# Squares summed ahead of their product, and norm and modulation steps in another order, in a two-block transformer kernel

## The chip, the cores and the metric

The kernel runs on one core of a Trainium2 chip. The metric is device microseconds for one execution of the whole program. The engines are named as the profile names them: PE (TensorE, matrix products), PEld (its weight loads), DVE (VectorE), ACT (ScalarE), POOL (GpSimd) and SP (the queue that issues most DMAs).

## The reference

Two transformer blocks run one after the other on one sequence of 512 tokens of width 1024. The change touches the first block only. Cut to what matters, it computes

```
mod = silu(c) @ w_ada + b_ada                      # 6 vectors of 1024: shift1, scale1, gate1, shift2, scale2, gate2
h   = rms_norm(x, g_norm1) * (1 + scale1) + shift1
proj = h @ w_in                                    # q, k, v of the stick-breaking heads; q, k, v, o, gates of the mLSTM
q, k = rms_norm per head of 64                     # 8 heads
y_sb = stick_breaking(q, k, v);  y_ml = mlstm(...)
x   = x + gate1 * (concat(y_sb, y_ml) @ w_out)
h2  = rms_norm(x, g_norm2) * (1 + scale2) + shift2
x   = x + gate2 * peer(h2)                         # scores, two top-k stages, 16384 experts with tables u and v

rms_norm(x, g) = x * rsqrt(mean(x*x) + eps) * g
```

## The kernel before

The residual `xT` is held transposed: 8 tiles of 128 features by 512 tokens. Products keep float32 accuracy by splitting each operand into a rounded part and a rest: `cut` makes `whi` (a cast, mostly on ACT, L151) and `wlo` (a subtraction on DVE or POOL, L152) from a weight tile of 128x1024, `split` does the same to an activation, and `mm3` issues three products (L171 with `wlo`, L172 with the rest of the activation, L173 with both rounded parts). So a product that uses a weight tile waits for both its `whi` and its `wlo`.

A norm needs the sum of squares over the features, which lie on partitions: `square` (L1145, L1146) squares one tile on ACT and multiplies it by a matrix of ones on PE, which adds up the partitions and, over the 8 tiles, the features in one PSUM bank. `rstd` (from L192) then does one step from PSUM on DVE (L198, `rs_m`), a Ln and an Exp on ACT (L199, L200), and three steps on DVE (L203 to L205). With `split=True` the last three are handed back as a function, to be called later.

Everything the change touches lies inside `manual_schedule` sections, in which the order of the program text is the order that was chosen by hand for each engine's queue. Three stretches matter.

**The start** (`start`, 0 to 110 us). `silu(c)` is spread over partitions by 8 small products with a diagonal (`dg`, L1210) and copied to `cs` by ACT (L1213). Then come the 8 squares and their products, the cut of the first weight tile, and two `dot`s on DVE (L1195) that multiply a row tile of `w_ada` with `cs` and give 128 elements of scale and 128 of shift. Then a loop over the 8 feature tiles i runs:

```
fetch(i + 2)          # two tiles of w_ada, one of i_qk (SP)
dot(KD + i + 1)       # DVE, scale of the next tile
low(i)                # DVE, hl: the rest of the normed tile i
dot(i + 1)            # DVE, shift of the next tile
shape(i + 1)          # DVE: 2 small steps and mt; ACT: hh; then the next cut: ACT whi, POOL wlo
24 products of tile i # PE
```

`low(i)` needs `hh` of tile i, which ACT makes from `mt`. After the loop, 96 products give the values of the heads, in 8 groups `kk`; between the groups `normed` norms one tile of q or k each, in the order 0, 4, 1, 5, 2, 6, 3, 7: a product with a block matrix (L1280), `rs_m` on DVE, Ln and Exp on ACT, and a group later `finish` (L203 to L205 and L1285 on DVE). As soon as tiles 0 and 4 are done, `stack(0)` splits the first two heads into the operands of their scores: 4 copies on ACT, 2 on DVE, 4 subtractions on POOL (L1351 to L1355). The values are copied out of PSUM by ACT at the end (L1312, `vs`), and the stick-breaking section begins with the score products `z` (L1444).

**The end of the mixer** (`mlstm`, 378 to 407 us). 8 projections of `w_out` (`project("b", ...)`), each 12 products; in turn with them DVE does the dots of shift2 and scale2 (L1134) and adds each result to `xT` (L1639), ACT and PE do `square`, and POOL makes the `wlo` of the next weight tiles. At the end `rstd` makes the second norm's factor.

**The start of the routing** (`peer` and `route`, from 407 us). `cut_u(0)` cuts the first tile of the expert table u (`whi` on DVE at L149, `wlo` on POOL). `modulated` (from L1148) norms and modulates the 8 tiles: per tile a multiplication on DVE (L1161, `mt`), two passes on ACT (L1162, L1163, the second gives `phh`), a copy of the first 128 tokens on POOL (L1165, `h2t`), and the rest `phl` on DVE (L1156). Then the loop over 16 query tiles begins. Its first round issues the products of query tile 0 feature by feature, and after every second feature pulls one piece of the expert products out of a queue of fillers:

```
for k in range(KD):
    c.mm3(ps, ...)            # query tile 0, feature k
    if i == 0 and k % 2:
        fill.pull(1)          # 6 products of tile u(0), with features k-1 and k
```

The functions that the diff touches, and what calls them:

Of the kernel before, what the change touches and what calls it, by code (L numbers as in the profile page):

```python
# [20 lines left out]
P = 128  # L21
# [1077 lines left out]
class Block1:  # L1099
# [48 lines left out]
    def modulated(self, rstd, gname, shift, scale, hi, lo, keep=None, bufs=2):  # L1148
# [5 lines left out]

        def low(k):
            nc.vector.tensor_tensor(out=lo[:, k], in0=ts[k], in1=hi[:, k].bitcast(F32), op=ALU.subtract)  # L1156

        for k in range(KD):
            t = self.sm.tile([P, S], F32, tag="mt", bufs=bufs, name=c.name("mt"))
            ts.append(t)  # L1160
            nc.vector.tensor_tensor(out=t, in0=self.xT[:, k], in1=rstd, op=ALU.mult)  # L1161
            nc.scalar.activation(t, t, AF.Identity, scale=a[:, k:k + 1], bias=self.mod[:, shift + k:shift + k + 1])  # L1162
            nc.scalar.copy(hi[:, k], t)  # L1163
            if keep is not None:
                nc.gpsimd.tensor_copy(keep[:, k], t[:, :P])  # L1165
            if k > 1:
                low(k - 2)
# [3 lines left out]
    def start(self, wk, hh, hl, q, k, vs, gq, stack):  # L1171
# [34 lines left out]
        cs = [self.bank() for _ in range(2)]  # L1206
        for j in range(KD):
            d = dg[:, j * P:(j + 1) * P]
            nc.vector.tensor_scalar(d, c.ident, ct[:, j:j + 1], None, op0=ALU.mult)
            mm(cs[j // 4][:, j % 4 * P:(j % 4 + 1) * P], lhsT=c.ones, rhs=d, start=j % 4 == 0, stop=True,  # L1210
               skip_group_check=True)
        for i in range(2):
# [4 lines left out]
        pn = self.bank()  # L1217
        for j in range(KD):
            self.square(pn, j)
# [5 lines left out]
        rstd = c.rstd(self.sm, pn, [P, S], D, EPS1, "hrstd", bufs=2)  # L1225
# [3 lines left out]
        def shape(i):  # L1229
            nc.vector.tensor_scalar(mod[:, KD + i:KD + i + 1], mod[:, KD + i:KD + i + 1], up[:, i:i + 1],  # L1230
                                    c.col("g1", i), op0=ALU.add, op1=ALU.mult)
            nc.vector.tensor_scalar(mod[:, i:i + 1], mod[:, i:i + 1], c.col("b_ada", i), None, op0=ALU.add)
            ts[i] = self.sm.tile([P, S], F32, tag="mt", name=c.name("mt"))
# [9 lines left out]

        shape(0)
        for i in range(KD):
            fetch(i + 2)
            if i + 1 < KD:
                dot(KD + i + 1)
                low(i)
                dot(i + 1)  # L1250
                shape(i + 1)
# [25 lines left out]
        def normed(j):  # L1277
# [6 lines left out]
            def finish():  # L1284
                nc.vector.scalar_tensor_tensor(out=dst[m], in0=dst[m], scalar=gq if m < 4 else c.col("gk"),  # L1285
                                               in1=rest(), op0=ALU.mult, op1=ALU.mult)
                if m == 4:
                    stack(0)
# [5 lines left out]
        for k0 in range(0, KD, 2):  # L1294
# [3 lines left out]
            for kk in range(k0, k0 + 2):  # L1298
                s0 = slice((kk - k0) * 512, (kk - k0 + 1) * 512)
                if kk % 2 == 0 and k0 + 2 < KD:  # L1300
                    vcut[k0 + 2] = c.cut(vraw.pop(k0 + 2), 1024, None, nc.gpsimd)
                for b in range(NB):
# [247 lines left out]
    def mlstm(self, m2, wk, big, hh, hl, vm, ym, qk, og, rows, identb, closing):  # L1550
# [200 lines left out]
        with self.psum(bank=7, norm=1):  # L1751
            pn = self.bank("norm")
            for m in range(KD):
# [4 lines left out]
                if m:  # L1758
                    self.square(pn, m - 1)
# [3 lines left out]
            self.square(pn, KD - 1)  # L1763
            self.rstd = c.rstd(self.sm, pn, [P, S], D, EPS1, "prstd", self.st, bufs=2)

    def peer(self):
# [7 lines left out]
        with ExitStack() as ctx:  # L1774
# [62 lines left out]
            with tc.manual_schedule():  # L1837
                fetch_u(1)
                cut_u(0)
# [550 lines left out]
```

## Time and profile before

| what | value |
|---|---|
| median of 3 runs | 3176.5 us (3174.7 to 3179.04) |
| the profiled execution's own time | 3176.89 us |
| its span in the profile | 3175.0 us |
| PE busy | 2967.8 us, 93% of the span |
| DVE busy | 2143.1 us, 67% |
| ACT busy | 1289.8 us, 41% |
| POOL busy | 662.1 us, 21% |

The profile is of one execution. Its span runs from the first to the last instruction, and the execution's own time adds what lies around it. Busy shares are means over very different stages: the stretches that the change touches are less than 200 us of the span, and what counts in them is which wait ends last. In a timeline each line gives the start, the duration, the engine, the line, the operation, the tiles, and in brackets how long the engine had stood idle and whom it waited for; an operation that is held up after it was issued shows a longer duration instead.

### The profile page before, as it was taken

The numbers are of one execution on the slowest core, as the hardware profiler recorded it, in microseconds if no ns is written. First come the engines' busy times: TensorE is split into PE (matmuls) and PEld (weight loads), VectorE is DVE, ScalarE is ACT, GpSimd is POOL, SyncE is SP. The second block draws the span as 40 slices with busy tenths as digits, with TensorE's granted clock in tenths as the row PEclk, the third lists the DMA queues.
The fourth block names the chain that finished last, engine by engine and source line by source line (L and its number), as shares of the span: only waits on it lengthen the run. The fifth ranks groups of instructions, "written<-read, shape, count | busy, mean of one in ns | idle before, by whom it ended". The sixth has DMA issues, their size and how long they took to land.

```text
span 3175.0 us, 44359 instructions
## 1 busy us (share of the span) xinstructions
PE 2967.8 (93%) x17073; PEld 2588.8 (82%) x17073; DVE 2143.1 (67%) x4089; ACT 1289.8 (41%) x2356; POOL 662.1 (21%) x453
## 2 busy tenths in 40 slices
PE   8889987858999999999999999989999988999998
PEld 6666577758899999999998777689999966798896
DVE  6886667789777778777786647755445666555454
ACT  3764342237533333333333334433233367433232
POOL 4432134630112112111110234330000322300001
PEclk9989899879999999999999999999999999899999
DMA  6222321215888888888887311022232311122322
GB/s 217 73 74 100 105 88 67 77 50 220 327 312 301 320 304 302 317 305 311 307 290 241 106 60 41 30 72 94 81 100 81 99 33 34 54 87 86 101 88 85
DMA packets 160805, 479.29 MB, mean 151 GB/s; under 512 B 13489, under 2 KB 68657, under 8 KB 142546
## 3 DMA queue, kind: packets, MB, share of 16 engines
q1 hardware_dynamic: 139346, 316.03, 29.9%
q0 software_dynamic: 18432, 134.23, 11.4%
q10 hardware_dynamic: 2816, 26.22, 2.0%
q8 instruction: 134, 2.20, 0.3%
q14 instruction: 77, 0.63, 0.1%
HBM read 449.15 MB, written 27.27 MB: 150 GB/s over the span
## 4 chain that ended last, share of the span: by engine, by line
PE 72%; DVE 14%; issue 6%; POOL 3%; ACT 3%; DMA 1%; SPq 0%; DVEq 0%; POOLq 0%; ACTq 0%
PE big L171 8%; PE big L173 8%; PE big L172 8%; PE y L172 5%; PE y L173 5%; PE y L171 5%; PE u L171 5%; PE u L173 5%; PE u L172 5%; POOL wlo L152 2%; PE bank L2233 2%; PE s L536 1%; PE f L171 1%; PE bank L172 1%; PE bank L171 1%
## 5 line engine op out<-in xcount | busy, mean ns | idle before, releaser
L152 DVE TENSOR_TENSOR wlo<-wraw,whi 128x1024 fp32r<-128x1024 f32 (+2 forms) x409 | 479.6, 1173 | 531.6 <-ACT whi L151 528.8
L151 ACT CAST whi<-wraw 128x1024 fp32r<-128x1024 f32 (+3 forms) x530 | 524.3, 989 | 702.3 <-PE y L173 267.6
L171 PE MATMUL big<-xh,wlo 128*128 128x264 f32 (+2 forms) x1408 | 422.5, 300 | 4.8 <-POOL wlo L152 4.5
L173 PE MATMUL big<-xh,whi 128*128 128x264 f32 (+2 forms) x1408 | 420.6, 299 | 0.0
L172 PE MATMUL big<-xl,whi 128*128 128x264 f32 (+2 forms) x1408 | 419.8, 298 | 0.0
L152 POOL TENSOR_TENSOR wlo<-wraw,whi 128x1024 fp32r<-128x1024 f32 (+4 forms) x122 | 270.6, 2220 | 689.7 <-ACT whi L151 652.1
L171 PE MATMUL u<-phh,wlo 128*128 128x384 f32 x1024 | 353.7, 345 | 57.3 <-POOL wlo L152 33.2
L173 PE MATMUL u<-phh,whi 128*128 128x384 f32 x1024 | 349.8, 342 | 0.0
L172 PE MATMUL u<-phl,whi 128*128 128x384 f32 x1024 | 349.6, 341 | 0.0
L1887 POOL DMA_INDIRECT g<-in_uv,idx x128 | 159.9, 1249 | 819.0 <-DVE yg L1901 451.1
L173 PE MATMUL y<-whi,ph 128*128 128x512 f32 x768 | 301.1, 392 | 0.0
L172 PE MATMUL y<-wlo,ph 128*128 128x512 f32 x768 | 300.9, 392 | 0.0
L171 PE MATMUL y<-whi,pl 128*128 128x512 f32 x768 | 299.1, 389 | 1.5 <-DVE pl L167 1.5
L171 PEld LDWEIGHTS big<-xh,wlo 128*128 128x128 f32 x1408 | 266.6, 189 | 15.2 <-POOL wlo L152 6.0
L172 PEld LDWEIGHTS big<-xl,whi 128*128 128x128 f32 x1408 | 267.1, 190 | 8.1
L173 PEld LDWEIGHTS big<-xh,whi 128*128 128x128 f32 x1408 | 266.5, 189 | 7.8
L171 PEld LDWEIGHTS u<-phh,wlo 128*128 128x128 f32 x1024 | 198.0, 193 | 67.4 <-POOL wlo L152 38.0
L172 PEld LDWEIGHTS u<-phl,whi 128*128 128x128 f32 x1024 | 197.6, 193 | 4.3
L173 PEld LDWEIGHTS u<-phh,whi 128*128 128x128 f32 x1024 | 196.9, 192 | 0.0
L171 PE MATMUL big<-ah,wlo 128*128 128x264 f32 (+2 forms) x539 | 171.4, 318 | 1.9 <-DVE wlo L152 1.7
L172 PE MATMUL big<-al,whi 128*128 128x264 f32 (+2 forms) x539 | 170.8, 317 | 0.0
L173 PE MATMUL big<-ah,whi 128*128 128x264 f32 (+2 forms) x539 | 170.8, 317 | 0.0
(503 smaller groups left out, 6305.6 us busy)
## 6 DMA issues: line engine op xcount, KB each, us to landing
wraw<-in_ut SPq DMA_DIRECT2D x128, 512.0 KB, 6.0
wraw<-in_uv SPq DMA_DIRECT2D x128, 512.0 KB, 5.7
wraw<-in_f_in SPq DMA_DIRECT2D x88, 512.0 KB, 3.3
gscratch<-stage ACTq DMA_DIRECT2D x12, 2048.0 KB, 6.8
gt<-gscratch SPq DMA_DIRECT2D x32, 768.0 KB, 8.3
wada<-in_w_ada SPq DMA_DIRECT2D x40, 512.0 KB, 3.6
wraw<-in_f_out SPq DMA_DIRECT2D x32, 384.0 KB, 3.1
wraw<-in_f_out SPq DMA_DIRECT2D x32, 320.0 KB, 2.9
```

Of the source, the lines that this page charges most:

```text
L151: self.nc.scalar.copy(hi[:, :n], raw[:, :n])
L152: (engine or self.nc.vector).tensor_tensor(out=lo[:, :n], in0=raw[:, :n], in1=hi[:, :n].bitcast(F32), op=ALU.subtract)
L171: mm(out, lhsT=wl, rhs=xh, start=first, stop=False)
L172: mm(out, lhsT=wh, rhs=xl, start=False, stop=False)
L173: mm(out, lhsT=wh, rhs=xh, start=False, stop=last)
L536: mm(o[:, :n], lhsT=q[:, rows(b)], rhs=k[:, k0:k0 + n], start=True, stop=True)
L1887: nc.gpsimd.indirect_dma_start(out=g, out_offset=None, in_=t["uv"], in_offset=bass.IndirectOffsetOnAxis(ap=idx[:, k:k + 1], axis=0))
L2233: nc.tensor.matmul(ps[:, e * P:(e + 1) * P], lhsT=b[:, e], rhs=a[:, e], start=e == 0, stop=True, skip_group_check=True)
```

## The change

- In `start`, the squares come ahead of the copies of `cs`, in pairs: POOL adds the two squares of a pair, and PE multiplies the 4 sums by the ones instead of 8 squares, each product standing between the small products of `dg`.
- Still in `start`, the two small steps of `shape` become `scales`; those of tile 0 come ahead of `rstd`; and `low(i)` comes ahead of both dots instead of between them.
- `stack(0)` moves from the finish of tile 4 to the beginning of value group `kk == 5`.
- At the end of the mixer POOL adds 7 of the 8 squares into one tile, and PE does two products at the very end instead of 8 spread over the projections. The last three steps of `rstd` are handed to `modulated`.
- `modulated` takes the scale into the first multiplication on DVE and the shift into the pass that makes `hi` and into the step that makes `lo`: one pass on ACT less for each tile. The copy `h2t` moves from POOL to ACT.
- `cut_u(0)` moves from ahead of `route` to behind `modulated`.

```
--- before.py
+++ after.py
@@ -1152,17 +1152,22 @@
                                        op0=ALU.add, op1=ALU.mult)
         ts = []
 
+        def bias(k):
+            return self.mod[:, shift + k:shift + k + 1]
+
         def low(k):
-            nc.vector.tensor_tensor(out=lo[:, k], in0=ts[k], in1=hi[:, k].bitcast(F32), op=ALU.subtract)
-
+            nc.vector.scalar_tensor_tensor(out=lo[:, k], in0=ts[k], scalar=bias(k), in1=hi[:, k].bitcast(F32),
+                                           op0=ALU.add, op1=ALU.subtract)
+
+        rstd = rstd()
         for k in range(KD):
             t = self.sm.tile([P, S], F32, tag="mt", bufs=bufs, name=c.name("mt"))
             ts.append(t)
-            nc.vector.tensor_tensor(out=t, in0=self.xT[:, k], in1=rstd, op=ALU.mult)
-            nc.scalar.activation(t, t, AF.Identity, scale=a[:, k:k + 1], bias=self.mod[:, shift + k:shift + k + 1])
-            nc.scalar.copy(hi[:, k], t)
+            nc.vector.scalar_tensor_tensor(out=t, in0=self.xT[:, k], scalar=a[:, k:k + 1], in1=rstd,
+                                           op0=ALU.mult, op1=ALU.mult)
+            nc.scalar.activation(hi[:, k], t, AF.Identity, bias=bias(k))
             if keep is not None:
-                nc.gpsimd.tensor_copy(keep[:, k], t[:, :P])
+                nc.scalar.activation(keep[:, k], t[:, :P], AF.Identity, bias=bias(k))
             if k > 1:
                 low(k - 2)
         low(KD - 2)
@@ -1204,32 +1209,41 @@
         nc.vector.tensor_tensor(out=ct, in0=ct, in1=e, op=ALU.mult)
         dg = wk.tile([P, 1280], F32, tag="sw", bufs=2, name="dg")
         cs = [self.bank() for _ in range(2)]
+        pn = self.bank()
+        pairs = []
         for j in range(KD):
+            if j % 2 == 0:
+                pairs.append(self.sm.tile([P, S], F32, tag="mt", name=c.name("mt")))
+                nc.scalar.activation(pairs[-1], self.xT[:, j], AF.Square)
+            else:
+                sq = self.sm.tile([P, S], F32, tag="sq", name=c.name("sq"))
+                nc.scalar.activation(sq, self.xT[:, j], AF.Square)
+                nc.gpsimd.tensor_tensor(out=pairs[-1], in0=pairs[-1], in1=sq, op=ALU.add)
             d = dg[:, j * P:(j + 1) * P]
             nc.vector.tensor_scalar(d, c.ident, ct[:, j:j + 1], None, op0=ALU.mult)
             mm(cs[j // 4][:, j % 4 * P:(j % 4 + 1) * P], lhsT=c.ones, rhs=d, start=j % 4 == 0, stop=True,
                skip_group_check=True)
+            if j % 2:
+                mm(pn, lhsT=c.ones, rhs=pairs[-1], start=j == 1, stop=j == KD - 1)
         for i in range(2):
             nc.scalar.copy(self.cs[:, i * 512:(i + 1) * 512], cs[i])
         self.crow = self.dram.tile([1, D], F32, name="crow")
         nc.sync.dma_start(self.crow, self.cs[0:1, :])
         fetch(1)
-        pn = self.bank()
-        for j in range(KD):
-            self.square(pn, j)
         up = self.sm.tile([P, KD], F32, tag="up", bufs=1, name="up")
         nc.vector.tensor_scalar(up, c.col("b_ada", KD, KD), 1.0, None, op0=ALU.add)
         wcut[0] = c.cut(wraw.pop(0), D, None, nc.gpsimd)
         dot(KD)
         dot(0)
-        rstd = c.rstd(self.sm, pn, [P, S], D, EPS1, "hrstd", bufs=2)
         ts = {}
         outs = [self.bank() for _ in range(KD)]
 
-        def shape(i):
+        def scales(i):
             nc.vector.tensor_scalar(mod[:, KD + i:KD + i + 1], mod[:, KD + i:KD + i + 1], up[:, i:i + 1],
                                     c.col("g1", i), op0=ALU.add, op1=ALU.mult)
             nc.vector.tensor_scalar(mod[:, i:i + 1], mod[:, i:i + 1], c.col("b_ada", i), None, op0=ALU.add)
+
+        def shape(i):
             ts[i] = self.sm.tile([P, S], F32, tag="mt", name=c.name("mt"))
             nc.vector.scalar_tensor_tensor(out=ts[i], in0=self.xT[:, i], scalar=mod[:, KD + i:KD + i + 1], in1=rstd,
                                            op0=ALU.mult, op1=ALU.mult)
@@ -1241,13 +1255,16 @@
             nc.vector.scalar_tensor_tensor(out=hl[:, i], in0=ts.pop(i), scalar=mod[:, i:i + 1],
                                            in1=hh[:, i].bitcast(F32), op0=ALU.add, op1=ALU.subtract)
 
+        scales(0)
+        rstd = c.rstd(self.sm, pn, [P, S], D, EPS1, "hrstd", bufs=2)
         shape(0)
         for i in range(KD):
             fetch(i + 2)
             if i + 1 < KD:
+                low(i)
                 dot(KD + i + 1)
-                low(i)
                 dot(i + 1)
+                scales(i + 1)
                 shape(i + 1)
             else:
                 low(i)
@@ -1284,8 +1301,6 @@
             def finish():
                 nc.vector.scalar_tensor_tensor(out=dst[m], in0=dst[m], scalar=gq if m < 4 else c.col("gk"),
                                                in1=rest(), op0=ALU.mult, op1=ALU.mult)
-                if m == 4:
-                    stack(0)
             return finish
 
         late, todo = None, list(order)
@@ -1299,6 +1314,8 @@
                 s0 = slice((kk - k0) * 512, (kk - k0 + 1) * 512)
                 if kk % 2 == 0 and k0 + 2 < KD:
                     vcut[k0 + 2] = c.cut(vraw.pop(k0 + 2), 1024, None, nc.gpsimd)
+                if kk == 5:
+                    stack(0)
                 for b in range(NB):
                     sl = slice(b * P, (b + 1) * P)
                     c.mm3(tiles[b], hh[:, kk, sl], hl[:, kk, sl], wh[:, s0], wl[:, s0], kk == 0, kk == KD - 1)
@@ -1750,18 +1767,32 @@
             add()
         with self.psum(bank=7, norm=1):
             pn = self.bank("norm")
+            acc = wk.tile([P, S], F32, tag="cu", name=c.name("sqsum"))
+
+            def squared(m):
+                if m == 0:
+                    nc.scalar.activation(acc, self.xT[:, m], AF.Square)
+                    return
+                sq = self.sm.tile([P, S], F32, tag="sq", name=c.name("sq"))
+                nc.scalar.activation(sq, self.xT[:, m], AF.Square)
+                if m < KD - 1:
+                    nc.gpsimd.tensor_tensor(out=acc, in0=acc, in1=sq, op=ALU.add)
+                return sq
+
             for m in range(KD):
                 if m % 2 == 0:
                     hi, lo = w.take(("b", m // 2))
                 last = project("b", 4, m, hi, lo)
                 next(mods)
                 if m:
-                    self.square(pn, m - 1)
+                    squared(m - 1)
                 last()
             next(mods)
             self.wq = {i: w.take(("q", i)) for i in range(2)}
-            self.square(pn, KD - 1)
-            self.rstd = c.rstd(self.sm, pn, [P, S], D, EPS1, "prstd", self.st, bufs=2)
+            sq = squared(KD - 1)
+            mm(pn, lhsT=c.ones, rhs=acc, start=True, stop=False)
+            mm(pn, lhsT=c.ones, rhs=sq, start=False, stop=True)
+            self.rstd = c.rstd(self.sm, pn, [P, S], D, EPS1, "prstd", self.st, True, 2)
 
     def peer(self):
         c, nc, t, tc = self.c, self.c.nc, self.c.t, self.c.tc
@@ -1836,8 +1867,7 @@
             fill = Filler(ahead())
             with tc.manual_schedule():
                 fetch_u(1)
-                cut_u(0)
-                self.route(hh, hl, tok, gate, ef, fill)
+                self.route(hh, hl, tok, gate, ef, fill, cut_u)
                 nc.vector.tensor_copy(idx, ef[:, 0])
                 gep.append(ctx.enter_context(tc.tile_pool(reuse_waits="tile", name="ge2", bufs=STAGES[1] - STAGES[0])))
                 ahead_u["by"] = nc.vector
@@ -2009,7 +2039,7 @@
         for b in range(NB):
             v.max_index(idx[:, b, 8:16], vals[:, b, 8:16], rest[:, b])
 
-    def route(self, hh, hl, tok, gate, ef, fill):
+    def route(self, hh, hl, tok, gate, ef, fill, cut_first):
         c, nc, t, tc = self.c, self.c.nc, self.c.t, self.c.tc
         with ExitStack() as ctx:
             pre = self.sm = ctx.enter_context(tc.tile_pool(reuse_waits="tile", name="pre", bufs=2))
@@ -2026,6 +2056,7 @@
             wcut = self.wq
             h2t = pre.tile([P, KD, P], F32, tag="h2t", bufs=1, name="h2t")
             self.modulated(self.rstd, "g2", 24, 32, hh, hl, h2t, 4)
+            cut_first(0)
             iota = pre.tile([P, NCAND, PE_K], BF, tag="iota", bufs=1, name="iota")
             nc.gpsimd.iota(iota, pattern=[[1, NCAND], [0, PE_K]], base=0, channel_multiplier=0,
                            allow_small_or_imprecise_dtypes=True)
```

## Rows read from the trace of the kernel before

**Rows 1.** Busy time by stretch: window, its length, busy us (instructions) by engine, granted clock, DMA.
```profile
40.00:56.00 16.00, 15.97 (x68) 12.29 (x67) 16.00 (x23) 3.77 (x5) 10.29 (x3) 1.00 0.71 222
...
86.00:95.00 9.00, 2.53 (x8) 1.44 (x7) 8.85 (x7) 5.73 (x9) 8.12 (x5) 0.78 0.00 0
95.00:98.00 3.00, 3.00 (x9) 2.34 (x8) 2.97 (x2) 0.03 (x1) 2.79 (x1) 0.52 0.50 175
```

**Rows 2.** Timeline of the start, 0 to 25 us: ACT, DVE, POOL, PE.
```profile
9.42 0.58 ACT L1213 COPY cs<-bank 128x512 f32<-128x512 f32 x1 [1.02 <-PE bank L1210]
...
11.97 1.23 DVE L1195 SCALAR_TENSOR_TENSOR junk<-wada,cs 128x1024 bf16<-128x1024 f32 x1 [4.88 <-DMA wada<-in_w_ada]
...
18.01 2.35 POOL L152 TENSOR_TENSOR wlo<-wraw,whi 128x1024 fp32r<-128x1024 f32 x1 [13.78 <-ACT whi L151]
...
24.23 0.77 PE L171 MATMUL bank<-hh,wlo 128*128 128x512 f32 x1 [6.12 <-ACT hh L1236]
```

**Rows 3.** Timeline of one round of the start's loop, DVE.
```profile
32.93 1.21 DVE L1195 SCALAR_TENSOR_TENSOR junk<-wada,cs 128x1024 bf16<-128x1024 f32 x1
...
34.07 0.74 DVE L1241 SCALAR_TENSOR_TENSOR hl<-mt,mod,hh 128x512 fp32r<-128x512 f32 x1
34.74 1.21 DVE L1195 SCALAR_TENSOR_TENSOR junk<-wada,cs 128x1024 bf16<-128x1024 f32 x1
...
36.19 2.56 DVE L1234 SCALAR_TENSOR_TENSOR mt<-hT,mod,rs_y 128x512 f32<-128x512 f32 x1
```

**Rows 4.** Timeline of the same round, ACT and POOL.
```profile
33.04 0.73 ACT L1236 ACTIVATE hh<-mt,mod 128x512 fp32r<-128x512 f32 x1 [4.09 <-DVE mt L1234]
...
34.79 3.41 POOL L152 TENSOR_TENSOR wlo<-wraw,whi 128x1024 fp32r<-128x1024 f32 x1 [2.33 <-ACT whi L151]
```

**Rows 5.** Timeline of the value products and the head norms, 86 to 110 us.
```profile
88.33 1.62 POOL L1354 TENSOR_TENSOR sk<-sk__101,sk 64x512 fp32r<-64x512 f32 x1
...
88.86 1.64 DVE L205 SCALAR_TENSOR_TENSOR rs_y<-rs_m,rs_y 128x512 f32<-128x512 f32 x1
...
94.43 0.79 PE L172 MATMUL bank<-wlo,hh 128*128 128x512 f32 x1 [6.47 <-POOL wlo L152]
...
106.92 0.69 DVE L198 TENSOR_SCALAR rs_m<-bank 128x512 f32<-128x512 f32 x1
...
108.85 2.03 ACT L1312 COPY vs<-bank 128x512 f32<-128x512 f32 x4
...
109.95 0.50 PE L1444 MATMUL z<-sq,sk 128*128 128x512 f32 x1 [0.34 <-ACT vs L1312]
```

**Rows 6.** POOL's groups by form: line, shapes, count, busy us, mean ns, idle before.
```profile
L358 POOL TENSOR_TENSOR acc<-acc,sq 128x528 f32<-128x528 f32 x30 | 47.9, 1597 | 588.7 <-ACT sq L355 588.7
```

**Rows 7.** Timeline of the mixer's end: DVE, PE.
```profile
378.61 2.53 DVE L1134 SCALAR_TENSOR_TENSOR junk<-wada,cs 128x1024 bf16<-128x1024 f32 x1
...
400.67 1.02 PE L1146 MATMUL norm<-sq,ones 128*128 128x512 f32 x2
```

**Rows 8.** Timeline of the start of the routing, 407 to 428 us, DVE.
```profile
407.30 0.69 DVE L198 TENSOR_SCALAR rs_m<-norm 128x512 f32<-128x512 f32 x1 [0.49 <-PE norm L1146]
407.91 0.68 DVE L149 CAST whi<-wraw 128x1024 fp32r<-128x1024 f32 x1
...
409.35 2.21 DVE L203 TENSOR_TENSOR rs_m<-rs_m,rs_y 128x512 f32<-128x512 f32 x1 [0.68 <-ACT rs_y L200]
...
413.05 1.90 DVE L1161 TENSOR_TENSOR mt<-hT,prstd 128x512 f32<-128x512 f32 x3
```

**Rows 9.** The same stretch, PE and POOL.
```profile
418.41 0.50 PE L171 MATMUL u<-phh,wlo 128*128 128x384 f32 x1
...
427.24 0.93 PE L2129 MATMUL bank<-ident,h2t 128*128 128x128 f32 x7
...
414.66 0.44 POOL L1165 COPY h2t<-mt 128x128 f32<-128x128 f32 x1 [3.63 <-ACT mt L1162]
...
424.49 1.04 POOL L2030 IOTA iota<- 128x800 bf16 x1
```

More of the change, by code (lines that the diff above doesn't have):

```diff
@@ L1206, in start @@
         cs = [self.bank() for _ in range(2)]
+        pn = self.bank()
+        pairs = []
         for j in range(KD):
+            if j % 2 == 0:
+                pairs.append(self.sm.tile([P, S], F32, tag="mt", name=c.name("mt")))
+                nc.scalar.activation(pairs[-1], self.xT[:, j], AF.Square)
+            else:
+                sq = self.sm.tile([P, S], F32, tag="sq", name=c.name("sq"))
+                nc.scalar.activation(sq, self.xT[:, j], AF.Square)
+                nc.gpsimd.tensor_tensor(out=pairs[-1], in0=pairs[-1], in1=sq, op=ALU.add)
             d = dg[:, j * P:(j + 1) * P]
@@ L1211, in start @@
                skip_group_check=True)
+            if j % 2:
+                mm(pn, lhsT=c.ones, rhs=pairs[-1], start=j == 1, stop=j == KD - 1)
         for i in range(2):
@@ L1224, in start, with scales @@
         dot(0)
[L1225 removed]
         ts = {}
         outs = [self.bank() for _ in range(KD)]
[L1229 removed]
+        def scales(i):
             nc.vector.tensor_scalar(mod[:, KD + i:KD + i + 1], mod[:, KD + i:KD + i + 1], up[:, i:i + 1],
@@ L1232, in shape @@
             nc.vector.tensor_scalar(mod[:, i:i + 1], mod[:, i:i + 1], c.col("b_ada", i), None, op0=ALU.add)
+        def shape(i):
             ts[i] = self.sm.tile([P, S], F32, tag="mt", name=c.name("mt"))
@@ L1247, in start @@
             if i + 1 < KD:
+                low(i)
                 dot(KD + i + 1)
-                low(i)
                 dot(i + 1)
+                scales(i + 1)
                 shape(i + 1)
@@ L1301, in start @@
                     vcut[k0 + 2] = c.cut(vraw.pop(k0 + 2), 1024, None, nc.gpsimd)
+                if kk == 5:
+                    stack(0)
                 for b in range(NB):
@@ L1752, in mlstm, with squared @@
             pn = self.bank("norm")
+            acc = wk.tile([P, S], F32, tag="cu", name=c.name("sqsum"))
+            def squared(m):
+                if m == 0:
+                    nc.scalar.activation(acc, self.xT[:, m], AF.Square)
+                    return
+                sq = self.sm.tile([P, S], F32, tag="sq", name=c.name("sq"))
+                nc.scalar.activation(sq, self.xT[:, m], AF.Square)
+                if m < KD - 1:
+                    nc.gpsimd.tensor_tensor(out=acc, in0=acc, in1=sq, op=ALU.add)
+                return sq
             for m in range(KD):
@@ L1838, in peer @@
                 fetch_u(1)
-                cut_u(0)
-                self.route(hh, hl, tok, gate, ef, fill)
+                self.route(hh, hl, tok, gate, ef, fill, cut_u)
                 nc.vector.tensor_copy(idx, ef[:, 0])
@@ L2010, in top, with route @@
             v.max_index(idx[:, b, 8:16], vals[:, b, 8:16], rest[:, b])
-    def route(self, hh, hl, tok, gate, ef, fill):
+    def route(self, hh, hl, tok, gate, ef, fill, cut_first):
         c, nc, t, tc = self.c, self.c.nc, self.c.t, self.c.tc
```

30 lines of the change are left out of this document (17 added, 13 removed).

## The prediction

> **What bounds the kernel now.** I read the mean shares on the page first, and set them aside: PE is nearly always the engine that ends last, so an edit counts only where PE stands still, or will. The busy times by stretch, then the timelines, give three different pictures for the three places.
>
> In the loop of the start PE is busy 15.97 of 16 us, and so is DVE, 16.00 [rows 1]. The round is closed by a ring: `mt`, `hh`, the cut's `whi`, `wlo` on POOL, and the next `mt`. The reader should see in [rows 3, 4] that `wlo` is asked for at 34.79, while a dot runs on DVE (34.74, 1.21), and takes 3.41 where it takes 2.35 alone [rows 2]; and that `mt`, issued at 36.19, takes 2.56 where its neighbour `hl`, of the same shape, takes 0.74. Each waits until the other's instruction is over: `wlo` runs from the dot's end at 35.9 to 38.2, `mt` ends 0.55 later at 38.75. The previous `mt` ended just ahead of `hh` at 33.04, so a round takes 5.7 us.
>
> In the value products PE stands 6.47 us for `wlo` [rows 5], queued on POOL behind the four subtractions of `stack(0)`, and then does 9 products in 3.00 us at a granted clock of 0.52 [rows 1], the lower of its two levels (1.2 against 2.4 GHz): some 1.5 us more lost. But over the same time DVE is busy too, 8.85 of 9.00 and 2.97 of 3.00 us [rows 1].
>
> From the second norm's `rs_m` at 407.30 to the first products of the routing PE has nothing to do; at 409.35 L203 takes 2.21 because the `wlo` of u(0) holds it [rows 8].
>
> **The first product of the start.** The copies of `cs` move behind eight squares on ACT and, on PE, behind products that wait for POOL's sums; the last copy started at 9.42 [rows 2]. A sum on POOL has no row at 128x512; the nearest, 128x528, has a mean of 1.60 [rows 6]. No row tells when `xT` lands. If it comes early, the copy starts near 13, both dots (11.97 and on, before) are over ahead of `wlo`, and the first product, 24.23 [rows 2], comes about 2 us earlier, since nothing is left between the norm and `mt`. If the copy comes near 14.6, the first `whi` follows it, POOL takes the port at the end of the first dot, the second dot waits 2.35 us, and the product comes 1.8 later. I take 1.0 later, nearer to the second, as `wlo` got in behind the dot in [rows 4].
>
> **`low` ahead of the dots.** Before, a dot runs while ACT makes `hh`. After, DVE stands until `hh` is there, 0.8 us behind `mt`; then `low` (0.67 from issue to issue, 34.07 to 34.74) and the first dot (1.15) bring it to 2.6 us. `wlo` is asked for 1.75 after `hh` starts, as before [rows 4], so during that first dot, and runs behind it from 2.6 to 4.95. Now a whole dot, and not only `mt`, waits behind it: dot to 6.05, two small steps 0.3, `mt` to 7.05. The round grows from 5.7 to about 7.05, 1.35 us. PE had nothing spare, so it shows as PE waiting. Six rounds have `wlo` in them, 8.1; the first has none and loses the 0.8; less about 0.9 for what PE could spare and for the last round, which has no dots: 8.0 later. If DVE's second dot wins over the waiting `wlo`, the round is 6.65 and the loss 5.5; if neither waited, DVE's own 4.75 would hide behind PE and the loss be 0. The alternation of POOL (1.62) and DVE (1.64) in [rows 5], each waiting once for the other, speaks for the first.
>
> The Trainium skill (SBUF — State Buffer, SBUF: two separate sides) says that VectorE and GpSimd share one pair of ports under an exclusive lock, that a VectorE operation with two SBUF inputs needs it, and that whichever starts first holds it for its whole instruction. It does not say who is next when both wait: by its rule alone the loss in the loop lies between 5.5 and 8.0, by the rows at 8.0. It speaks against every POOL sum that this change adds beside a dot.
>
> **`stack(0)` later.** The stall of 6.47 and the slow 1.5 go: `wlo` is no longer behind the subtractions. What is late next: PE would be at `z` near 102 instead of 109.95 [rows 5], but `z` needs banks that ACT's copies `vs` empty, and these are queued behind the Ln and Exp of the last head norm, 1.93 us after its `rs_m` (106.92 to 108.85 [rows 5]). That `rs_m` is the end of a DVE queue that was full: eight norms of five steps each, and the same POOL subtractions and cuts between them, none of which goes. Working the queue through with each POOL operation holding one DVE operation brings the last `rs_m` to 106.1: 0.8 earlier. So the stall moves from the middle of the value products to `z`, slow clock and all. Bounds: nothing, and 8.0 (6.47 + 1.5), if DVE were not the pace.
>
> **Sums of squares at the mixer's end.** PE loses six of eight products of about 0.9 (1.02 for the pair of passes, overlapping the next [rows 7]), 5.2 us at most. Against it stand six POOL sums of 1.3 to 1.6 in a stretch where a dot is already held (378.61, 2.53 [rows 7]): eight dots of 1.15, six sums, two `wlo` of 2.35 on POOL and two of 1.2 on DVE have to take turns, some 25 us from 380 on, so the sixth sum ends near 405 and the last product near 407. I take 0, with 5 earlier and 2 later as bounds.
>
> **The second norm and `modulated`.** From `rs_m` to the first `mt` it was 5.75 us (407.30 to 413.05); L203 was held 1.5 of them. With the cut gone from there it is 4.25. Per tile ACT does one pass less and a small copy more, POOL no copy: ACT is no longer the pace, and DVE does 16 operations of 0.67, 10.7 us.
>
> **`cut_u(0)` behind `modulated`.** The first round of the routing needs u(0) after two features: u's products begin at 418.41 [rows 9], 11.1 us after `rs_m`. After, its `whi` on DVE (0.68 [rows 8]) comes behind all 16 operations and `wlo` on POOL (2.35) behind that: 4.25 + 10.7 + 0.1 + 0.7 + 0.1 + 2.35 = 18.2 us after `rs_m`. PE waits in order, with two features done. From u's first product to the transposes it took 8.8 us (to 427.24 [rows 9]), and all of that work is still there; after the wait 1.5 more go to the lower clock, as in the value products. Together 7.1 + 1.5 = 8.6 later. Bounds: 7, and, if the cut is not held back, 1.7 earlier. Everything in the routing hangs on query tile 0, so nothing absorbs it.
>
> **The sum.** 1.0 + 8.0 - 0.8 + 0 + 8.6 = 16.8 us, on the profiled execution's 3176.9 (span 3175.0 and 1.9 around it), which lies 0.4 above the median of the runs: 3193.3, about 3193. A measurement of this kernel can tell about 0.2%, 6.4 us, from no change.
>
> **The rivals.**
>
> *The round of the loop does not grow.* POOL and DVE do not meet, or PE hides it. For it: with `hl` earlier, PE's second product waits less. Against: [rows 3, 4]. Then 3193.3 - 8.0, about 3185.
>
> *The stall in the value products is really gone.* For it: the chain of work ran through that POOL queue. Against: DVE's full queue. 8.0 in place of 0.8: 3186.
>
> *Only the loop loses.* The cut of u(0) runs early: 10.3 less, 3183.
>
> *Faster: queues are not in the order written.* Ready instructions go ahead. For it: the `whi` of u(0) and its neighbour at 407.91 ran ahead of L203 at 409.35, which the text has before them [rows 8]. Against: those stand in two different sections; inside `route` POOL stood 3.63 us for `h2t` at 414.66 and did the `iota`, which waits for nothing, only at 424.49, behind all eight copies [rows 9], as written. If the mechanism holds inside sections too, dots fill DVE's gap, the cut fills the wait for Exp, `vs` goes ahead of the last norm. Then both losses (8.0 and 10.3) and the 1.0 vanish, and with 1.7 in the routing and 5 at `z` the time is 3170. It decides from the point at which the cut's `whi` comes ahead of the first `mt`.
>
> *It does not do what it says.* The six products saved would show nothing, as I already take; alone it changes no sign.
>
> **How the numbers follow.** The forecast, both losses: 0.55. The loop's loss missing 0.15, the stall gone 0.10, the loop alone 0.08, the order by readiness 0.12. Slower by over 0.2% (above 3182.9): 0.55 + 0.13 + 0.08 and half of the loop alone, less the ends of the bounds: 0.77. Within: 0.12. Faster: 0.11, nearly all from the last rival. The likeliest case alone runs from 3187 to 3199; 8 in 10 reach down over the middle cases to 3179.
>
> **What would show it.** In the profile after: one of the two dots in each round at 2.3 us or more, where all took 1.21, and PE waiting for `wlo` or `hh` in each round; no wait at L172 in the value products, but one of some 7 us at `z` for `vs`; POOL's sums at the mixer's end alternating with dots held up, and `rs_m` not earlier than the shift of what lies ahead of it; L203 at 0.7; PE waiting some 9 us for the `wlo` of u(0) after 6 products of query tile 0. The prediction is wrong if the cut of u(0) stands early on DVE, if the rounds stay at 5.7, or if the last head norm comes much earlier than DVE's queue allows.

## The result, and the profile after

The changed kernel takes 3193.65 us (median of 5 runs, 3191.71 to 3202.63) against 3176.5 for the kernel before (5 runs beside them): ratio 1.0058, 95% interval 1.0046 to 1.0069, or 14.6 to 21.9 us more. The forecast was 3193. Its profiled execution took 3194.35 (span 3192.6); the landmarks below are from it, set against the execution that the rows ahead of the prediction are from.

The views are read in the same order as before. First the busy times by stretch (window, length, busy us and instructions of PE, PEld, DVE, ACT, POOL, granted clock, DMA), of the changed kernel:

```profile
50.00:66.00 16.00, 13.05 (x55) 10.14 (x56) 14.34 (x21) 3.33 (x4) 6.72 (x3) 1.00 0.56 193
...
112.30:120.70 8.40, 0.31 (x2) 0.03 (x1) 8.16 (x12) 4.06 (x8) 1.94 (x2) 0.84 0.19 62
120.70:123.70 3.00, 3.00 (x13) 2.72 (x14) 2.90 (x4) 1.34 (x2) 1.59 (x1) 0.50 0.03 5
```

In the loop neither PE nor DVE is full any more: 13.05 and 14.34 of 16 us, where both were [rows 1]. After the value products, which now run without the stall, PE stands still for 8 us, and the 3 us behind that, the first of `z`, run at the lower clock. The same 3 us of the kernel before were at the full one:

```profile
109.95:112.95 3.00, 3.00 (x18) 2.17 (x19) 2.90 (x5) 3.00 (x4) 1.05 (x1) 1.00 0.02 5
```

The timeline of the start of the changed kernel (start, duration, then engine, line, operation, tiles; in brackets the idle time before it and what ended that), POOL, PE, ACT, DVE:

```profile
7.60 1.26 POOL L1221 TENSOR_TENSOR mt<-mt,sq 128x512 f32<-128x512 f32 x1 [6.52 <-ACT sq L1220]
8.95 3.06 POOL L1363 TENSOR_SCALAR sql<-jp 64x512 fp32r<-64x512 int32 x2
11.99 2.47 POOL L1221 TENSOR_TENSOR mt<-mt,sq 128x512 f32<-128x512 f32 x2
...
13.29 1.13 PE L1227 MATMUL bank<-mt,ones 128*128 128x512 f32 x2 [1.44 <-POOL mt L1221]
...
14.45 0.63 ACT L1217 ACTIVATE mt<-hT 128x512 f32<-128x512 f32 x1 [2.28 <-PE bank L1227]
...
15.51 1.28 ACT L1229 COPY cs<-bank 128x512 f32<-128x512 f32 x2
...
18.09 3.24 DVE L1200 SCALAR_TENSOR_TENSOR junk<-wada,cs 128x1024 bf16<-128x1024 f32 x1
...
27.49 0.77 PE L171 MATMUL bank<-hh,wlo 128*128 128x512 f32 x1 [9.37 <-ACT hh L1250]
```

Two pads of `ql` on POOL, 3.06 us, stand between the first and the second sum. Before the change they ran at 1.17, when POOL had nothing else to do. The seventh square, on ACT at 14.45, waits 2.28 for a product that waited for a sum, and the copies of `cs` stand behind it at 15.51, where the last one started at 9.42 [rows 2].

One round of the loop, DVE, ACT and POOL:

```profile
37.84 0.74 DVE L1248 SCALAR_TENSOR_TENSOR mt<-hT,mod,rs_y 128x512 f32<-128x512 f32 x1
39.37 0.75 DVE L1255 SCALAR_TENSOR_TENSOR hl<-mt,mod,hh 128x512 fp32r<-128x512 f32 x1 [0.79 <-ACT hh L1250]
40.04 1.22 DVE L1200 SCALAR_TENSOR_TENSOR junk<-wada,cs 128x1024 bf16<-128x1024 f32 x1
...
41.30 3.27 DVE L1200 SCALAR_TENSOR_TENSOR junk<-wada,cs 128x1024 bf16<-128x1024 f32 x1
...
44.81 0.74 DVE L1248 SCALAR_TENSOR_TENSOR mt<-hT,mod,rs_y 128x512 f32<-128x512 f32 x1
...
38.62 0.72 ACT L1250 ACTIVATE hh<-mt,mod 128x512 fp32r<-128x512 f32 x1 [5.32 <-DVE mt L1248]
...
40.36 3.13 POOL L152 TENSOR_TENSOR wlo<-wraw,whi 128x1024 fp32r<-128x1024 f32 x1 [3.84 <-ACT whi L151]
```

DVE stands 0.79 for `hh`, the first dot runs while `wlo` waits (40.36 asked for, 3.13 in all), and the second dot waits for `wlo`: 3.27 where a dot takes 1.22. `mt` is 0.74 now, where it was 2.56 [rows 3]. From one `mt` to the next (37.84 to 44.81) it is 6.97 us.

The value products, `z`, the mixer's end and the routing:

```profile
117.15 0.68 DVE L198 TENSOR_SCALAR rs_m<-bank 128x512 f32<-128x512 f32 x1
...
119.06 2.03 ACT L1329 COPY vs<-bank 128x512 f32<-128x512 f32 x4
...
120.70 0.77 PE L1461 MATMUL z<-sq,sk 128*128 128x512 f32 x1 [8.09 <-DVE ym L1302]
...
123.88 1.24 ACT L1472 ACTIVATE su<-z 128x1280 f32<-128x1280 f32 x1 [1.84 <-PE z L1464]
...
396.41 2.71 DVE L1134 SCALAR_TENSOR_TENSOR junk<-wada,cs 128x1024 bf16<-128x1024 f32 x1
...
397.99 6.74 POOL L1779 TENSOR_TENSOR sqsum<-sqsum,sq 128x512 f32<-128x512 f32 x3
...
406.99 1.12 PE L1793 MATMUL norm<-sqsum,ones 128*128 128x512 f32 x2 [3.14 <-POOL sqsum L1779]
...
411.80 0.69 DVE L203 TENSOR_TENSOR rs_m<-rs_m,rs_y 128x512 f32<-128x512 f32 x1 [1.36 <-ACT rs_y L200]
...
424.59 0.69 DVE L149 CAST whi<-wraw 128x1024 fp32r<-128x1024 f32 x1
...
427.75 0.69 PE L171 MATMUL u<-phh,wlo 128*128 128x384 f32 x1 [8.43 <-POOL wlo L152]
```

`z` waits 8.09 us. It is put down to `ym`; the third of the copies `vs` ends at about the same time, 120.6. At the mixer's end a sum takes 2.25 where the first sum of the start, alone, took 1.26, and dots are held. L203 is 0.69 again, where it was 2.21 [rows 8]. The `whi` of u(0) comes behind all of `modulated`, and PE waits 8.43 us for its `wlo`.

### The profile page after: what moved, and what is told of

It is laid out like the page before. It is cut to its first block, busy times and chain, and to the rows that moved or that the text cites. A ratio compares the mean times of both kernels' runs of the same rounds, so it can differ in the third digit from the quotient of the medians.

```text
span 3192.6 us, 44324 instructions
## 1 busy us (share of the span) xinstructions
PE 2954.6 (93%) x17053; PEld 2581.4 (81%) x17053; DVE 2158.4 (68%) x4089; ACT 1286.8 (40%) x2356; POOL 672.3 (21%) x455
## 4 chain that ended last, share of the span: by engine, by line
PE 68%; DVE 15%; issue 8%; POOL 4%; ACT 3%; DMA 1%; SPq 0%; DVEq 0%; POOLq 0%; ACTq 0%
PE big L171 8%; PE big L173 8%; PE big L172 8%; PE y L173 5%; PE y L172 5%; PE y L171 5%; PE u L171 5%; PE u L173 5%; PE u L172 5%; POOL wlo L152 2%; PE s L536 1%; PE bank L2264 1%; POOL pr L2126 1%; PE f L171 1%; PE f L173 1%
## 5 line engine op out<-in xcount | busy, mean ns | idle before, releaser
L358 POOL TENSOR_TENSOR acc<-acc,sq 128x528 f32<-128x528 f32 x30 | 48.1, 1605 | 588.6 <-ACT sq L355 588.6
```

The source lines that it names most:

```text
L358: nc.gpsimd.tensor_tensor(out=self.acc, in0=self.acc, in1=sq, op=ALU.add)
```

## The experiments

Each kernel's median stands beside that of the kernel before in the same comparison (3177.04 to 3177.7).

**The loop alone put back** (x_dots): the changed kernel with the dots around `low` as before.

```
-                low(i)
                 dot(KD + i + 1)
+                low(i)
                 dot(i + 1)
```

> The changed kernel with the dots of the start's loop in the order of before (dot, low, dot). Theory of the prediction: the round falls back from 6.97 to 5.75 us, no dot is held, the copies of q and k come 7.7 us earlier than in the changed kernel, and the whole lies near 3186 us. Rival: what is gained ahead of 300 us is absorbed there, as the shift fell from 10.6 to 4.3 us between 300 and 378 us in the changed kernel: then the rounds are as short, but the time is only 1 to 3 us below the changed kernel, 3191 or more.

3188.33 us (5 runs), ratio 1.0041 (1.0028 to 1.0055): 5.3 less than the changed kernel. Its timeline, DVE and POOL, has the held `mt` back, and from one `mt` to the next it is 5.75 us:

```profile
39.84 1.22 DVE L1200 SCALAR_TENSOR_TENSOR junk<-wada,cs 128x1024 bf16<-128x1024 f32 x1
...
41.29 2.57 DVE L1248 SCALAR_TENSOR_TENSOR mt<-hT,mod,rs_y 128x512 f32<-128x512 f32 x1
...
39.89 3.42 POOL L152 TENSOR_TENSOR wlo<-wraw,whi 128x1024 fp32r<-128x1024 f32 x1 [2.33 <-ACT whi L151]
```

The end of the loop (last copy of `k`) comes at 77.58 in place of 83.43, and it is 48.3 us behind the loop's first product, where the changed kernel takes 55.9. What stands on DVE behind the held `wlo` decides: a short step that everything needs, or a whole dot and then that step.

**The cut of u(0) alone put back** (x_cut): ahead of the routing, as before.

```
                 fetch_u(1)
+                cut_u(0)
                 self.route(hh, hl, tok, gate, ef, fill, cut_u)
...
-            cut_first(0)
```

> The changed kernel with the cut of u(0) back ahead of the routing. Theory of the prediction: no wait of PE for u's first wlo (8.4 us in the changed kernel), L203 of the second norm held again by 1.5 us, in all 8.6 us less, near 3185 us. Rival: the routing is paced by POOL and DVE and gives the time back, so that the first top-k moves by 8.6 us and the end by less than 4.

3186.76 us (5 runs), 1.0039 (1.0025 to 1.0053): 6.9 less. From `rs_m` to the first MAX8 of the routing it takes 30.1 us, as before, where the changed kernel takes 38.6. L203 pays for it again, held by the cut on POOL:

```profile
412.07 0.69 DVE L198 TENSOR_SCALAR rs_m<-norm 128x512 f32<-128x512 f32 x1 [1.46 <-PE norm L1794]
...
414.12 2.21 DVE L203 TENSOR_TENSOR rs_m<-rs_m,rs_y 128x512 f32<-128x512 f32 x1 [0.68 <-ACT rs_y L200]
...
422.95 0.52 PE L171 MATMUL u<-phh,wlo 128*128 128x384 f32 x1
```

**Both put back** (x_both): the two edits above together.

> Both undone, the other parts of the change kept. If the two add up: 7.7 + 8.6 less than the changed kernel, near 3177 us, the same as the kernel before within its uncertainty. If the first is absorbed: near 3183.

3178.18 us (11 runs), 1.0003 (0.9994 to 1.0012). The two account for nearly the whole loss; all that is left of the change comes to nothing that the times can tell. Only the pair is well clear of the noise: against the kernel before, the changed kernel lies 14.6 to 21.9 us higher, x_dots 8.9 to 17.5 and x_cut 7.9 to 16.8, which overlap, and this one -1.9 to 3.8. How the loss divides between the two is read from the profiles.

**The stacking alone** (b_stack): the kernel before with `stack(0)` moved.

```
-                if m == 4:
-                    stack(0)
...
+                if kk == 5:
+                    stack(0)
```

> The kernel before with nothing but the stacking of the first heads moved to value group 5. Theory of the prediction: the wait of 6.47 us at the value products goes, one of some 7 us at the first score product comes, because DVE's queue of head norms ends where it did; the time is the same within 1.5 us. Rival: DVE is not the pace, the score product comes 6 to 8 us earlier, and the time is near 3169.

3176.85 us (11 runs), 1.0001 (0.9991 to 1.0012). The wait in the value products is gone and stands at `z`:

```profile
108.97 0.76 PE L1444 MATMUL z<-sq,sk 128*128 128x512 f32 x1 [7.61 <-ACT vs L1312]
```

**The pads off POOL** (a_pad): the changed kernel, the two pads issued on DVE.

```
-                nc.gpsimd.tensor_scalar(ql[pad, e], ...)
+                nc.vector.tensor_scalar(ql[pad, e], ...)
```

> The changed kernel with the two pads of ql (L1363) issued on DVE instead of POOL. Theory: the first product of the loop comes 3.3 us later than before (27.49 against 24.23, where I had 1.0) because POOL did these pads, 3.06 us, between its first and its second sum of squares, and the squares, the copies of cs and the dots waited behind them. Then without them on POOL the second sum starts near 9, the first dot near 14, and the first product stands at 24.5 to 26; nothing else changes, so the time is some 2 us less than the changed kernel's 3193.65. Rival: the sums and the products at the lower clock set the pace, pads or not; then the first product stays at 27 or later.

```profile
9.09 1.27 POOL L1221 TENSOR_TENSOR mt<-mt,sq 128x512 f32<-128x512 f32 x1 [0.55 <-ACT sq L1220]
...
14.87 0.58 ACT L1229 COPY cs<-bank 128x512 f32<-128x512 f32 x1 [1.07 <-PE bank L1224]
...
16.75 3.24 DVE L1200 SCALAR_TENSOR_TENSOR junk<-wada,cs 128x1024 bf16<-128x1024 f32 x1
...
26.16 0.77 PE L171 MATMUL bank<-hh,wlo 128*128 128x512 f32 x1 [10.32 <-ACT hh L1250]
```

A miss by a little: the second sum starts at 9.09 as expected, but the first product comes only 1.3 earlier, 1.9 later than before. The rest of the 3.3 is the late copy and the held second dot. The 1.3 is one reading: in the five profiles that have the pads on POOL (the changed kernel twice, x_dots, x_cut, x_both) the first product came between 27.20 and 29.26. In two of them, at 27.20 and 27.49, the second pair's product was about as fast as here (1.13 and 1.12 against 1.02), and against these the pads cost 1.0 to 1.3. The time, 3196.78 (4 runs, 1.0049 to 1.0082), shows no gain; 1.3 us is below what it can tell.

**A later start** (b_delay): the kernel before with nine dots more ahead of the first two.

```
+        for _ in range(9):
+            ...   # the same dot(KD), its result overwritten
         dot(KD)
         dot(0)
```

> The kernel before, with nine more dots (1.15 us each, the same operands, results overwritten by the dot that stands there anyway) on DVE ahead of the first two: nothing but a later start, about 10.4 us. It asks where the 6.3 us went that the changed kernel makes up between 300 and 378 us with the same instructions and waits at a higher granted clock. Theory: the clock of that stretch depends on when the kernel gets there, not on the edits; then the delay gives back 3 to 6 us there as well (split of ml to the last og below 74 us, where the kernel before has 76.5), and the time is 3181 to 3185. Rival: it comes from an edit; then the stretch keeps 76.5 us and the time is near 3187.

3183.45 us (10 runs), 1.0017 (1.0007 to 1.0027); the first product is 9.15 later (33.38), and the stretch keeps its 76.5 us. Neither theory holds whole: the time is the first one's, the stretch the rival's. And the time, 2.2 to 8.6 us more, lies just below the 8.8 us that the profile's span has grown.

**The mixer's end alone** (b_end): the kernel before with the squares added on POOL.

```
-                    self.square(pn, m - 1)
+                    squared(m - 1)
...
-            self.square(pn, KD - 1)
+            sq = squared(KD - 1)
+            mm(pn, lhsT=c.ones, rhs=acc, start=True, stop=False)
+            mm(pn, lhsT=c.ones, rhs=sq, start=False, stop=True)
```

> The kernel before with the mixer's end alone as in the change: squares added on POOL, two products in place of eight (the second norm, the modulated step and the cut of u(0) as before). Theory: the last og to rs_m shrinks from 36.1 us to about 34 (the changed kernel has 34.25), and the stretch from 300 to 378 stays as it is, 76.5 us, since what lies ahead of it comes at the same time; so about 2 us faster, 3174 to 3175. Rival: the gain of 300 to 378 hangs on this edit; then split of ml to the last og is near 71 to 73 us and the time about 3170. Second rival: the products saved show nothing and rs_m stays at 407.3.

3178.29 us (10 runs), 1.0007 (0.9997 to 1.0016). In the profile the last `og` to `rs_m` took 33.5 us where it was 36.1, and the stretch ahead of the edit 69.9 where it was 76.5, as the rival had it. The times moved by neither.

**Three controls**: the kernel before (b_again), the mixer's end alone (b_end2) and the changed kernel (a_again), each once more and unchanged, one execution each: 3177.28, 3177.95 and 3202.22 us.

> The kernel before once more, unchanged, for a second profile of it: a control on how far the granted clock of one execution can be trusted. Theory: the 300 to 378 us stretch is the same in every execution of these instructions (76.5 us from the split of ml to the last og in all three kernels without the mixer's end edit), so it shows 76.5 again, and its first product near 24.2. Rival: the clock of a stretch changes from one execution to the next, and the stretch shows 70 to 74 us, or the first product is 1 us or more off; then what I counted as a gain of the edit is no effect of it.

> The kernel before with the mixer's end edit alone, once more, unchanged: the control from the other side. Theory: the stretch that took 69.9 us there takes 70 to 73 again, as in all seven kernels with this edit. Rival: it takes 76.5 this time; then the association was chance.

> The changed kernel once more, unchanged. It asks which of the differences from before belong to the change: the first product of the loop near 27.5, the loop's end (last copy of k) 56 us behind it, the last og to rs_m 34.2, rs_m to the first MAX8 38.6 should all come back within 0.3 us if they come from the order of work; the stretch from the split of ml to the last og, and the way from the first MAX8 to the first y product, 399.7 us (396.1 before), are those that the granted clock may move. Theory: the first four come back, the last two move by a few us. Rival: all come back, and the 6.3 us gained and the 3.5 us lost are effects of the change.

The mixer's end alone and the changed kernel both had 76.5 this time. The same eight products in it, in the two executions of the mixer's end alone and then in the two of the changed kernel:

```profile
303.55 2.43 PE L1630 MATMUL z<-mqk 128*128 128x512 f32 x8
```

```profile
304.05 4.64 PE L1630 MATMUL z<-mqk 128*128 128x512 f32 x8
```

```profile
314.36 2.43 PE L1647 MATMUL z<-mqk 128*128 128x512 f32 x8
```

```profile
318.52 4.64 PE L1647 MATMUL z<-mqk 128*128 128x512 f32 x8
```

Within each pair the instructions and their order are the same; the granted clock over these products is 1.00 in the first of the two and 0.50 in the second, and PE's last wait ahead of the first pair was 0.91 and 0.47 us. I had put the gain down to the time of arrival first, and then to the edit, since seven kernels with the mixer's end showed 69.9 to 73.2 and three without it 76.5. Neither is enough: the delay left the stretch as it was, and the same kernel shows both lengths. But the controls do not show what decides. They and best2, below, ran on another chip than the experiments before them (13 and 7 in the record), and there all four profiles have 76.5, three with the edit and one without. On chip 7 all six with the edit are short, and the two without are at 76.5. Whether the execution, the chip, or the edit on one of the chips makes the difference is open.

By stage, the two executions of the changed kernel against the two of the kernel before (us; the first pair of columns is the one the prediction's rows are from):

| stage | before | after | more | before again | after again | more |
|---|---|---|---|---|---|---|
| to the loop's first product | 24.23 | 27.49 | 3.26 | 24.49 | 29.07 | 4.58 |
| loop, to the last copy of `k` | 48.25 | 55.94 | 7.69 | 48.26 | 55.96 | 7.70 |
| to the first max step on `su` | 43.19 | 44.34 | 1.15 | 43.03 | 44.35 | 1.32 |
| to the split of `ml` | 179.00 | 177.52 | -1.48 | 179.19 | 179.80 | 0.61 |
| to the last `og` | 76.49 | 70.22 | -6.27 | 76.49 | 76.49 | 0.00 |
| to `rs_m` of the second norm | 36.14 | 34.24 | -1.90 | 36.11 | 33.74 | -2.37 |
| to the first MAX8 | 30.10 | 38.56 | 8.46 | 31.20 | 39.37 | 8.17 |
| to the first product of `y` | 396.13 | 399.66 | 3.53 | 395.52 | 397.71 | 2.19 |
| to the end of the span | 2341.5 | 2344.6 | 3.2 | 2341.1 | 2344.0 | 2.9 |

The theory of a_again was right in part: of the four that were to come back within 0.3 us only the loop did (0.02). The steps from `og` and `rs_m` came back within 0.5 and 0.8, the first product was 1.6 off. The last two rows came back too, 5 to 7 us together that no term has. They are not shown to come from the routing: the mixer's end alone, with the routing as before, also took 399.4 and 396.7 us in the first of them, in its two executions, and 2344.0 and 2343.5 in the second. Over all fourteen profiles the first of these rows goes with the mixer's end: 396.7 to 399.7 in the ten that have it, 395.3 to 396.1 in the four that do not. No run shows why.

**What pays, alone** (best1): the start, loop and stacking of before, with the two small steps on `mod` ahead of the norm; the mixer's end and the fused `modulated`; and the cut of u(0), `wlo` on DVE, between the norm's two halves.

```
+        if first is not None:
+            first()          # cut_u(0), whi and wlo on DVE
         rstd = rstd()
```

> Only what the runs so far show to pay: the start, the loop and the stacking of before (but the two small steps on mod ahead of the norm's steps, where DVE stands anyway), the mixer's end as in the change, and the second norm split with the cut of u(0) whole on DVE in the wait for the Exp, ahead of the rest of the norm. Theory: 0.3 us at the first product, 2 at the mixer's end, and rs_m to the first product of u below 10.5 us where it was 11.1 (no cut on POOL holds L203), so 2.5 to 4 us: 3172 to 3174.5. Rival: the gain of rs_m is given back behind it, in the routing, as the changed kernel lost 1.8 there that nothing explains; then 3176 to 3178.

3177.86 us (10 runs), 1.0001 (0.9990 to 1.0012). The routing does what was expected: the first product of u is 9.8 us after `rs_m`, where it was 11.1, and the first MAX8 29.2. But the first product of the loop came at 26.16. The norm's eight products, in the order of before, took 9.5 us there, where they took 7.5, as this stretch of best1 and then that of before show:

```profile
10.50:20.00 9.50, 9.32 (x16) 3.37 (x16) 2.77 (x6) 5.36 (x9) 0.00 (x0) 1.00 1.03 418
```

```profile
10.50:18.50 8.00, 7.52 (x16) 2.46 (x16) 2.82 (x5) 5.27 (x9) 0.49 (x1) 1.00 1.02 416
```

The granted clock is 1.00 in both, so the lower clock that the next expectation names is not what the rows show. b_delay has it too: there the same sixteen passes took 9.3, with only the work of DVE beside them changed, while all five profiles with the start of before have 7.5. The cause is open. The ten runs of best1 lie between 3169.67 and 3182.34.

**The same with pairs on DVE at the start** (best2):

```
+        dot(KD)
+        pair(2)      # two squares on ACT, their sum on DVE, one product
+        pair(3)
         dot(0)
```

> As best1 (the mixer's end of the change, the second norm split with the cut of u(0) whole on DVE in the wait for the Exp; the loop and the stacking of before), and at the start the squares added in pairs, as in the change, but on DVE around the first dot, with the copies of cs ahead of the squares as before: four products in place of eight, and POOL has no sum. Theory: the first product comes at 22.5 to 23.5 (24.23 before, 26.16 in best1, where the eight products ran at a lower clock), rs_m 2 us earlier beside that, the first MAX8 29.2 after rs_m: 3 to 4.5 us in all, 3172.5 to 3174. Rival: what is won ahead of the routing is lost behind it, as in best1 and in the mixer's end alone, whose medians did not move; then 3176 to 3178.5.

The cut fills the wait for Exp, and L203 is not held:

```profile
406.01 0.68 DVE L149 CAST whi<-wraw 128x1024 fp32r<-128x1024 f32 x1
406.73 1.23 DVE L152 TENSOR_TENSOR wlo<-wraw,whi 128x1024 fp32r<-128x1024 f32 x1
407.87 0.68 DVE L203 TENSOR_TENSOR rs_m<-rs_m,rs_y 128x512 f32<-128x512 f32 x1
```

3176.43 us (12 runs), 0.9993 (0.9983 to 1.0002). The first product missed, at 24.75: the third and fourth pair wait on ACT for PE's products (1.39 and 0.56), and the second dot stands ahead of the norm's `rs_m`. The first MAX8 is 3.5 earlier than before, but only 1.5 of that is left at the first product of `y`. At best it is level with the kernel before; it is not shown to be faster.

## Why the prediction came out, point by point

**The loop** (8.0): right, and by its mechanism: 7.7, a round of 6.97 where 7.05 was worked out, one dot of each round at 3.27. In the times it is 5.3 (x_dots), which alone is not clear of the noise. The alternation decided it: DVE's second dot did not go ahead of the waiting `wlo`, so the bound of 5.5 was not met. The Trainium skill (SBUF — State Buffer, SBUF: two separate sides) has VectorE and GpSimd exclude each other on their ports for a whole instruction; the trace agrees, with 3.27 and 3.13 for two operations that take 1.22 and 2.35 alone.

**`cut_u(0)` behind `modulated`** (8.6): right. The first product of u came 18.0 us after `rs_m` (18.2 worked out), the first MAX8 8.5 and 8.2 later. In the times 6.9 (x_cut). The second norm's 1.5 is there too: 4.23 from `rs_m` to the first `mt` (4.25 worked out), and 5.74 again with the cut put back.

**The first product** (1.0, with 1.8 as the late bound): this is the step that failed, by its size. I chose between two cases by when the copy of `cs` comes, near 13 or near 14.6. It came at 15.5, so the late case held, with the second dot behind `wlo`, and worse. I had priced the sums, but not what else POOL would have in its queue: the pads, which stood at 1.17 before, where no row that I took shows them. (The 13.78 us of idle ahead of `wlo` in [rows 2] begin at 4.23, where they ended.) They are 1.0 to 1.3 us (a_pad), and the late case itself is 1.9, as bounded. The second execution, with PE's pair products at 2.07 where the first had some at 1.13, was 4.6 later; the five profiles with this start have 27.2 to 29.3, five with the start of before 23.9 to 24.5. With 1.8 for the late case and 1.3 for the pads the term would have been 3.1.

**`stack(0)` later** (-0.8): the mechanism was right, the stall did move to `z`, and DVE's queue was the pace (-0.2 at `z` in the change, -0.7 in b_stack, both against the end of the loop). What the step left out is where the low clock goes. "Slow clock and all", it said, but in the value products those slow microseconds had been made up by the wait for DVE that followed; at `z` ACT's softmax steps wait for them (1.84 ahead of `su`). So the chain lost 1.2 us in place of winning 0.8.

**The mixer's end** (0, with 5 earlier and 2 later): 1.7 to 2.7 earlier in each of the ten profiles of a kernel that has it; inside the bounds. The sums do set the norm, as worked out (PE waits 3.14 for the last), and dots are held. But the sixth sum ended 31.4 us behind the last `og` (405.14 and 1.79, less 375.51), which is 402.6 in the time of the kernel before, where I had 405. In the times it does not show (b_end).

**The sum**: 16.8 against 17.15 in the medians. By stages that came back in both pairs, the terms are 3.3 to 4.6, 7.7, 1.2, -2.1 and 8.3, some 19; the first product and the stack were counted too low by 4.3 to 5.6 together, and the mixer's end too high by 2. The closeness of 3193 to 3193.65 is partly luck: errors of opposite sign cancel, and single executions lie far apart. In the table above the spans of the first pair of executions differ by 17.6 us, those of the second by 25.1; the first had 6.3 us given back between the split of `ml` and the last `og`, at a granted clock of 0.92 where it was 0.84. Of the rivals, that the round does not grow, that the stall is gone, and that only the loop loses are excluded by rows; that queues are not in written order is excluded, for steps of one section, by the cut, which stood at 424.59 behind all of `modulated`.

What stays open: the 5 to 7 us behind the first MAX8 in both pairs, what set the clock between 300 and 378 us, and why 9.15 us of delay at the start cost only 2.2 to 8.6 in the times.

## What to carry to other kernels

When two engines take turns at their operands, ask what stands directly behind the waiting instruction on the engine that loses: the loop lost 1.2 us a round because a dot and not the short `mt` stood there. When a step is moved behind another, list all that its engine may then have to do, work of other parts too: the pads cost 1.0 to 1.3 us that I had not looked for. And a stretch of a single profile that changes ahead of the edit, or with the same instructions, is profiled a second time, on the same chip, before a cause is given to it.

## What the hardware showed that was not expected

The same instructions in the same order ran at another granted clock in a second execution: eight products of `z` took 2.43 us at 1.00 and 4.64 at 0.50, and the stretch around them 70.2 and 76.5 us in the same kernel. For the mixer's end alone the two executions were on two chips, and for the changed kernel the chip of the first is not on record, so it is not shown that the execution alone decides. On one chip the whole time of best1 went from 3169.67, at a mean granted clock of 0.971, to 3182.34 at 0.964: 0.4%, more than most edits here are worth. The start can differ as well at a granted clock of 1.00: on that same chip the sixteen passes of the first norm took 7.5 us in two profiles (b_end, b_stack) and 9.3 and 9.5 in two others (b_delay, best1), in which only DVE's work beside them is another. Why is not shown. The pads of `ql`, two at 64x512, took 3.06 us on POOL and 0.85 on DVE.
